# One copy for 1280 scores, another instruction for the second softmax's factor, and norm statistics on GpSimd in a differential-attention layer

## The chip, the cores and the metric

The kernel runs on one core of a Trainium2 chip. TensorE (PE) multiplies matrices into PSUM; its weight loads are listed as PEld. VectorE (DVE), ScalarE (ACT) and GpSimd (POOL) do the elementwise work, and SyncE (SP) issues the DMAs. The metric is the device time of one execution in microseconds (us).

## The reference

A trunk of two layers works on 1024 latent tokens and 256 context tokens of width 1024. Layer 0 mixes tokens with a Fourier transform, layer 1 with differential attention; each layer ends in a SwiGLU feed-forward. The change lies in the attention of layer 1, cut here to what matters:

```python
def diff_attn_core(q, k, v, lam):            # 8 heads, 2 components c of width 64; v has width 128
    s = einsum('bqhcd,bkhcd->bhcqk', q, k) * 64 ** -0.5
    p = softmax(s, axis=-1)                  # over 256 context and 1024 latent keys
    w = p[:, :, 0] - lam * p[:, :, 1]
    return einsum('bhqk,bkhe->bqhe', w, v)

def finish(o):
    o = rms_norm(o, subln_gain) * (1.0 - lam_init)
    return o.reshape(b, l, 1024) @ w_out
```

The subtracted weights are formed without a division of the whole row: with e0 and e1 the exponentials of the two components and r0, r1 their row sums, the kernel uses e0 - lam * (r0 / r1) * e1, which is w times r0. The RMS norm that follows takes r0 out again; its epsilon is therefore multiplied by r0 squared.

## The kernel before

The attention goes over 16 groups, each one head `h` and one half `qg` of the 1024 queries. A group has four query tiles `j` of 128 queries, and each tile has two units, one for each component `c`. `unit(j, c)` (L1006) lets PE write the scores of 128 queries against 1280 keys into PSUM: 1024 columns into a two-bank tile `sc` that rotates through two buffers, and, for both components of the tile at once, 256 columns each into the one bank of `ct`. DVE then copies the scores to SBUF with the sign turned, 1024 columns on L1017 and 256 on L1018; both are accumulating tensor_scalar instructions whose accumulator takes the row's minimum, and each is followed by a small instruction that reads the accumulator out. ACT takes the exponential of all 1280 columns in one instruction and sums the row (L1019).

After the second unit of a tile DVE works out the factor: a reciprocal (L1022), then a scalar_tensor_tensor on a single column (L1023). The second exponential is multiplied by it, on POOL for the tiles in `POOLM` (L1029) and on ACT for the others (L1031), and POOL adds the two (L1032). In the first group the tiles in `RAMP` do both steps on DVE instead (L1025).

The second half of the work on a group runs in ten steps `kt` over the keys (L1184). PE transposes four 128x128 blocks of the weights into a bank `pt` (L1187), ACT and DVE split them into a high and a low part (L55, L56), and PE multiplies them with the values in three matmuls into `po` (L1191 to L1193). Units are issued ahead of this: `advance` (L1190) keeps them three, later five units ahead of the following group's start, so about one unit goes with each `kt`. After the last step `post` copies `po` out (L1046), transposes it back (L1051), copies it on DVE (L1053) and squares it on ACT (L1056), both from the same bank, multiplies epsilon by r0 squared on DVE (L1059), and, once for the two groups of a head, adds the two terms (L1067) and takes the inverse root in eleven small DVE instructions (L60 to L69). POOL then scales the outputs (L1071), and four more transposes (L1078) and an ACT copy (L1082) store them. For the last head each half does this by itself. `oproj0` overlaps the output projection of the first 512 tokens with the last group.

The order on each engine is made by the framework from the program order and its own estimates; a semaphore wait is set for each dependency. PSUM has eight banks of 512 float32 columns: four for the two `sc` buffers, one for `ct`, one for `po`, two for `pt`.

Of the kernel before, what the change touches and what calls it, by code (L numbers as in the profile page):

```python
# [20 lines left out]
P = 128  # L21
# [14 lines left out]
def trunk(tc, a, dbg=None, stop=99):  # L36
# [21 lines left out]
    def rsqrt_ops(y, v, t, steps=3):  # L58
        yi = y.bitcast(I32)
        V.tensor_scalar(yi, v.bitcast(I32), 1, None, op0=ALU.logical_shift_right)  # L60
        yield
        V.tensor_scalar(yi, yi, -1, 0x5F3759DF, op0=ALU.mult, op1=ALU.add)
        yield
        for _ in range(steps):
            V.tensor_tensor(out=t, in0=y, in1=y, op=ALU.mult)
            yield
            V.scalar_tensor_tensor(out=t, in0=t, scalar=-0.5, in1=v, op0=ALU.mult, op1=ALU.mult)
            yield
            V.scalar_tensor_tensor(out=y, in0=t, scalar=1.5, in1=y, op0=ALU.add, op1=ALU.mult)  # L69
            yield  # L70

    def run(*gens):
# [888 lines left out]
    ap = ph4.enter_context(tc.tile_pool(name="ap", bufs=2, reuse_waits="tile"))  # L961
    pss = ph4.enter_context(tc.tile_pool(name="pss", bufs=2, space=PSUM, reuse_waits="tile"))
    pst = ph4.enter_context(tc.tile_pool(name="pst", bufs=2, space=PSUM, reuse_waits="tile"))
# [11 lines left out]
    sg = cst.tile([P, 1], F32, name="sg")  # L975
    V.tensor_scalar(sg, subln, 1.0 - LAM_INIT, None, op0=ALU.mult)

    oT = {}
    pairs = {}
    NE, LEAD, POOLM, RAMP = (11, 3), 5, (1, 2, 3), (1, 3)  # L980

    def load_v(h):
        vs = ap.tile([P, 2, 10, P], F32R, name="v")
        for s in range(2):
            nc.sync.dma_start(r32(vs[:, s]), vD[s, :, h * P:(h + 1) * P].rearrange("(t p) e -> p t e", p=P))
        heads[h].append(vs)

    def qk_units(h, qg):
# [10 lines left out]
        es_ = {}  # L999
        ct = {}  # L1000

# [4 lines left out]
        def unit(j, c):  # L1006
            jsl = slice(j * P, (j + 1) * P)
            col = lambda i: st[:, i, j:j + 1]
            sc = pss.tile([P, 2, 512], F32, name="sc")
            for bk in range(2):  # L1010
                scores(sc[:, bk], c, jsl, slice(bk * 512, (bk + 1) * 512))
            if c == 0:
                ct[j] = pst.tile([P, 2, LC], F32, name="ct", bufs=1)
                for cc in range(2):
                    scores(ct[j][:, cc], cc, jsl, slice(L, T))
            e = ap.tile([P, T], F32, name=f"e{c}", bufs=NE[c])
            V.tensor_scalar(e[:, 0:L], sc.rearrange("p a b -> p (a b)"), -1.0, 3.0e38, op0=ALU.mult, op1=ALU.min, accum_out=col(c))  # L1017
            V.tensor_scalar(e[:, L:T], ct[j][:, c], -1.0, col(c), op0=ALU.mult, op1=ALU.min, accum_out=col(4 + c))  # L1018
            S.activation(out=e, in_=e, func=AF.Exp, scale=-1.0, bias=col(4 + c), accum_out=col(10 + c))  # L1019
            es_[c] = e  # L1020
            if c == 1:
                V.reciprocal(col(12), col(11))  # L1022
                V.scalar_tensor_tensor(out=col(12), in0=col(12), scalar=nlam, in1=col(10), op0=ALU.mult, op1=ALU.mult)  # L1023
                if (h, qg) == (0, 0) and j in RAMP:
                    V.scalar_tensor_tensor(out=es_[0], in0=es_[1], scalar=col(12), in1=es_[0], op0=ALU.mult, op1=ALU.add)  # L1025
                    wts[j] = es_[0]
                    return
                if j in POOLM:
                    G.tensor_tensor(out=es_[1], in0=es_[1], in1=col(12).broadcast_to([P, T]), op=ALU.mult)  # L1029
                else:  # L1030
                    S.activation(out=es_[1], in_=es_[1], func=AF.Copy, scale=col(12))  # L1031
                G.tensor_tensor(out=es_[0], in0=es_[0], in1=es_[1], op=ALU.add)  # L1032
                wts[j] = es_[0]

# [4 lines left out]
    def post(h, qg, po, st):  # L1039
# [8 lines left out]
        def p1():  # L1048
# [9 lines left out]
            z = sn[:, 1, 4 * qg:4 * qg + 4]  # L1058
            V.scalar_tensor_tensor(out=z, in0=st[:, 10], scalar=EPS, in1=st[:, 10], op0=ALU.mult, op1=ALU.mult)  # L1059
            if not both:  # L1060
# [4 lines left out]
        def norm(qs):  # L1065
            s0, s1, s2_, s3 = (sn[:, i, 4 * qs[0]:4 * qs[-1] + 4] for i in range(4))
            V.scalar_tensor_tensor(out=s0, in0=s0, scalar=1.0 / P, in1=s1, op0=ALU.mult, op1=ALU.add)  # L1067
            rsqrt(s2_, s0, s3)
            for q in qs:
# [29 lines left out]
    def advance(target):  # L1099
        nonlocal done  # L1100
        while done < target:
            if not stream:
                n = len(info)
                if n >= len(groups):
                    return
                need(n)
            stream.pop(0)()
            done += 1

    def oproj0():  # L1110
# [26 lines left out]
        for nn in range(NC):  # L1137
# [4 lines left out]
            if nn == 5:  # L1142
                for k in (5, 6):
                    os1(k)
                for i in range(2):
                    nc.sync.dma_start(xt1[i], xres[:, 4 * i:4 * i + 4, 512:1024])
            if nn % 2 == 0:
                acc = pss.tile([P, 2, 512], F32, name="acc", tag="sc")
            pt = acc[:, nn % 2]
            for k in range(NC):  # L1150
# [532 lines left out]
```

## Time and profile before

| | |
|---|---|
| median of three runs | 2795.62 us (2793.28 to 2798.28) |
| profiled execution | 2793.9 us, span of its instructions 2792.1 us |
| granted TensorE clock, mean over the span | 0.987 |
| busy over the span | PE 2664.8 (95%), PEld 2182.4 (78%), DVE 1609.0 (58%), ACT 1106.5 (40%), POOL 960.1 (34%) |
| first and last score copy (L1017) | 1538.6 and 1946.2 us |
| first and last value matmul (L1191) | 1563.8 and 1997.3 us |

The shares are means over stages with different limits; the attention is the only stage in which DVE, and not PE, is busy over nine tenths. Times below count from the span's start. A duration runs from an instruction's start to its end, and neighbours on an engine overlap a little, so the time that an instruction takes from its engine is read from start to start.

### The profile page before, as it was taken

Reading aid. Unit: us, or ns where it says so; the run is one execution under the profiler, and the core shown is the slowest. Engines: PE = TensorE matmul, PEld = TensorE weight load, DVE = VectorE, ACT = ScalarE, POOL = GpSimd, SP = SyncE. Lnnn points to the kernel's source line nnn. Section 1 sums busy time; section 2 is a strip of 40 time slices with the busy share of each in tenths; the row PEclk is TensorE's granted clock in tenths of the full one; section 3 lists DMA queues with packets and bytes.
Section 4 is the critical chain, followed back from the end, with each engine's and each line's share of the span. In section 5 each row is a group of like instructions: output and inputs, shape, how many; then the busy total and the mean of one; then the engine's idle time right before and its main releaser. Section 6 shows DMA issues by size and latency. Waiting matters only on the chain.

```text
span 2792.1 us, 35671 instructions
## 1 busy us (share of the span) xinstructions
PE 2664.8 (95%) x13234; PEld 2182.4 (78%) x13234; DVE 1609.0 (58%) x2920; ACT 1106.5 (40%) x1940; POOL 960.1 (34%) x648
## 2 busy tenths in 40 slices
PE   6999999999999999999999888898987999999999
PEld 4678888888888888878888666676766788888887
DVE  7744644434333434586764999999666555555342
ACT  5642333222322111333343776687434333334231
POOL 4431024221211000013351676777046666651000
PEclk9999999999999999999999999999999999999999
DMA  6682122222222111143335523222243222226352
GB/s 210 203 272 84 31 76 80 84 87 79 88 83 68 39 38 38 50 138 116 114 114 185 157 83 107 83 69 84 80 128 94 87 87 82 82 79 208 109 181 87
DMA packets 284480, 290.64 MB, mean 104 GB/s; under 512 B 16249, under 2 KB 201874, under 8 KB 284306
## 3 DMA queue, kind: packets, MB, share of 16 engines
q1 hardware_dynamic: 282146, 284.69, 32.8%
q0 software_dynamic: 2160, 3.67, 0.4%
q8 instruction: 104, 1.70, 0.3%
q14 instruction: 70, 0.57, 0.1%
HBM read 234.83 MB, written 53.48 MB: 103 GB/s over the span
## 4 chain that ended last, share of the span: by engine, by line
PE 71%; DVE 11%; issue 8%; POOL 6%; DMA 2%; ACT 2%; SPq 0%; POOLq 0%; DVEq 0%; ACTq 0%
PE ps L50 12%; PE ps L52 12%; PE ps L51 12%; PE b L1418 4%; PE b L1416 4%; PE b L1417 4%; PE b L51 3%; PE b L52 3%; PE b L50 3%; DVE e L1017 2%; POOL xn L894 2%; POOL t L895 2%; PE pt L1187 1%; PE ps L229 1%; DVE wt L56 1%
## 5 line engine op out<-in xcount | busy, mean ns | idle before, releaser
L50 PE MATMUL ps<-un,whl 128*128 128x512 f32 x1184 | 464.4, 393 | 1.4 <-ACT XT L592 1.2
L51 PE MATMUL ps<-un,whl 128*128 128x512 f32 x1184 | 461.3, 390 | 0.0
L52 PE MATMUL ps<-un,whl 128*128 128x512 f32 x1184 | 460.9, 389 | 0.0
L56 DVE TENSOR_TENSOR whl<-raw,whl 128x512 fp32r<-128x512 f32 x219 | 170.8, 793 | 271.2 <-ACT whl L55 270.5
L50 PEld LDWEIGHTS ps<-un,whl 128*128 128x128 f32 x1184 | 222.4, 188 | 54.9 <-issue 3.5
L52 PEld LDWEIGHTS ps<-un,whl 128*128 128x128 f32 x1184 | 222.3, 188 | 46.9
L51 PEld LDWEIGHTS ps<-un,whl 128*128 128x128 f32 x1184 | 222.6, 188 | 44.8 <-issue 0.7
L55 ACT ACTIVATE whl<-raw 128x512 fp32r<-128x512 f32 x219 | 134.7, 628 | 246.2 <-PE ps L52 178.1
L736 DVE SCALAR_TENSOR_TENSOR XT<-ps,mods,XT 128x512 f32<-128x512 f32 (+1 forms) x264 | 170.3, 660 | 85.2 <-PE ps L52 84.9
L262 POOL TENSOR_TENSOR acc<-acc,aw 128x512 f32<-128x512 f32 x84 | 112.6, 1340 | 296.4 <-ACT acc L258 231.2
L1032 POOL TENSOR_TENSOR e<-e,e 128x1280 f32<-128x1280 f32 x62 | 182.9, 2951 | 91.3 <-DMA q<-qD 52.8
L1019 ACT ACTIVATE e<-e,st 128x1280 f32<-128x1280 f32 x128 | 174.7, 1366 | 62.0 <-DVE e L1018 45.7
L607 POOL TENSOR_TENSOR nacc<-nacc,s 128x512 f32<-128x512 f32 (+1 forms) x35 | 41.0, 1172 | 414.2 <-ACT s L606 392.7
L51 PE MATMUL ps<-u,whl 128*128 128x256 f32 x592 | 167.5, 283 | 0.0
L52 PE MATMUL ps<-u,whl 128*128 128x256 f32 x592 | 167.4, 283 | 0.0
L50 PE MATMUL ps<-u,whl 128*128 128x256 f32 x592 | 167.3, 283 | 0.0
L1017 DVE TENSOR_SCALAR_CACHE_REDUCE e<-sc 128x1024 f32<-128x1024 f32 x128 | 154.8, 1216 | 10.3 <-PE sc L1004 8.1
L819 PE MATMUL ps<-whl,un 128*128 128x512 f32 x384 | 152.9, 398 | 0.0
L820 PE MATMUL ps<-whl,un 128*128 128x512 f32 x384 | 150.2, 392 | 1.0 <-DVE whl L56 0.9
L821 PE MATMUL ps<-whl,un 128*128 128x512 f32 x384 | 149.9, 391 | 0.0
L51 PE MATMUL b<-au,wu 128*128 128x512 f32 x336 | 130.9, 390 | 0.1
L50 PE MATMUL b<-au,wu 128*128 128x512 f32 x336 | 130.8, 390 | 0.0
(419 smaller groups left out, 6436.3 us busy)
## 6 DMA issues: line engine op xcount, KB each, us to landing
aw<-in_w_ada SPq DMA_DIRECT2D x96, 256.0 KB, 2.8
raw<-in_ffn_w_in SPq DMA_DIRECT2D x88, 256.0 KB, 2.9
wr<-in_ffn_w_out SPq DMA_DIRECT2D x42, 512.0 KB, 4.1
wada<-in_w_ada SPq DMA_DIRECT2D x48, 256.0 KB, 3.3
un<-in_w_ada SPq DMA_DIRECT2D x48, 256.0 KB, 4.5
raw<-in_diff_w_in SPq DMA_DIRECT2D x48, 256.0 KB, 3.5
rq<-in_ffn_w_in SPq DMA_DIRECT2D x24, 512.0 KB, 5.6
raw<-in_ffn_w_out SPq DMA_DIRECT2D x44, 256.0 KB, 2.9
```

Of the source, the lines that this page charges most:

```text
L50: PE.matmul(out, wh, mh, start=start, stop=False)
L51: PE.matmul(out, wh, ml, start=False, stop=False)
L52: PE.matmul(out, wl, mh, start=False, stop=stop)
L55: S.activation(out=hl[:, 0], in_=src, func=AF.Copy)
L56: (lo_eng or V).tensor_tensor(out=hl[:, 1], in0=src, in1=r32(hl[:, 0]), op=ALU.subtract)
L736: V.scalar_tensor_tensor(out=xs, in0=pt, scalar=gmod[c][:, nn:nn + 1], in1=xs, op0=ALU.mult, op1=ALU.add)
L819: PE.matmul(pt, hk[:, 0, tsl], ws[k][:, 0], start=k == 0, stop=False)
L820: PE.matmul(pt, hk[:, 0, tsl], ws[k][:, 1], start=False, stop=False)
L821: PE.matmul(pt, hk[:, 1, tsl], ws[k][:, 0], start=False, stop=k == NC - 1)
L1017: V.tensor_scalar(e[:, 0:L], sc.rearrange("p a b -> p (a b)"), -1.0, 3.0e38, op0=ALU.mult, op1=ALU.min, accum_out=col(c))
L1019: S.activation(out=e, in_=e, func=AF.Exp, scale=-1.0, bias=col(4 + c), accum_out=col(10 + c))
L1032: G.tensor_tensor(out=es_[0], in0=es_[0], in1=es_[1], op=ALU.add)
```

## The change

Scores and PSUM: the rotating tiles `sc` and `ct` go. One tile `sc2` of 2560 columns holds both components: component 0 in columns 0 to 1279, component 1 in 1280 to 2559. That is five banks, and the middle one holds the last 256 columns of component 0 and the first 256 of component 1. PE fills each half in three pieces that end at bank borders (`CUTS`), so a unit still has six matmuls. One DVE instruction copies all 1280 columns.

Factor: it is formed by an accumulating tensor_scalar with two per-row operands, followed by the reading of the accumulator, and no longer by a scalar_tensor_tensor. The whole combination of a tile (factor, product and sum) is put off until after the copy and the exponential of the next unit. `POOLM` goes from tiles 1, 2, 3 to tiles 0 and 2, so ACT multiplies two tiles of a group where it multiplied one.

Norm: the square of r0, its product with epsilon and the sum run on POOL, and so does the inverse root, as a chain of fourteen POOL instructions (`rsqrt_pool`); only the last half of the last head keeps the DVE version. The factor 1/128 moves into the constants.

`oproj0` takes its accumulators from banks 0, 1, 3 and 4 of `sc2`. No DMA is added, removed or moved.

```diff
+    def rsqrt_pool(y, v, t, steps=3):
+        G.tensor_scalar(y.bitcast(I32), v.bitcast(I32), -0.5, float(0x5F3759DF), op0=ALU.mult, op1=ALU.add)
+        G.tensor_scalar(v, v, -0.5, None, op0=ALU.mult)
+        for _ in range(steps):
+            G.tensor_tensor(out=t, in0=y, in1=y, op=ALU.mult)
+            G.tensor_tensor(out=t, in0=t, in1=v, op=ALU.mult)
+            G.tensor_scalar(t, t, 1.5, None, op0=ALU.add)
+            G.tensor_tensor(out=y, in0=y, in1=t, op=ALU.mult)
...
-    V.tensor_scalar(sg, subln, 1.0 - LAM_INIT, None, op0=ALU.mult)
+    V.tensor_scalar(sg, subln, (1.0 - LAM_INIT) * math.sqrt(P), None, op0=ALU.mult)
+    sc2 = pss.tile([P, 2 * T], F32, name="sc2")
+    CUTS = ((0, 512, 1024, T), (0, 256, 768, T))
...
-    NE, LEAD, POOLM, RAMP = (11, 3), 5, (1, 2, 3), (1, 3)
+    NE, LEAD, POOLM, RAMP = (11, 3), 5, (0, 2), (1, 3)
...
-            sc = pss.tile([P, 2, 512], F32, name="sc")
-            for bk in range(2):
-                scores(sc[:, bk], c, jsl, slice(bk * 512, (bk + 1) * 512))
-            if c == 0:
-                ct[j] = pst.tile([P, 2, LC], F32, name="ct", bufs=1)
-                for cc in range(2):
-                    scores(ct[j][:, cc], cc, jsl, slice(L, T))
+            sc = sc2[:, c * T:(c + 1) * T]
+            for k0, k1 in zip(CUTS[c], CUTS[c][1:]):
+                scores(sc[:, k0:k1], c, jsl, slice(k0, k1))
             e = ap.tile([P, T], F32, name=f"e{c}", bufs=NE[c])
-            V.tensor_scalar(e[:, 0:L], sc.rearrange("p a b -> p (a b)"), -1.0, 3.0e38, op0=ALU.mult, op1=ALU.min, accum_out=col(c))
-            V.tensor_scalar(e[:, L:T], ct[j][:, c], -1.0, col(c), op0=ALU.mult, op1=ALU.min, accum_out=col(4 + c))
-            S.activation(out=e, in_=e, func=AF.Exp, scale=-1.0, bias=col(4 + c), accum_out=col(10 + c))
+            V.tensor_scalar(e, sc, -1.0, 3.0e38, op0=ALU.mult, op1=ALU.min, accum_out=col(c))
+            S.activation(out=e, in_=e, func=AF.Exp, scale=-1.0, bias=col(c), accum_out=col(10 + c))
             es_[c] = e
+            while comb:
+                comb.pop()()
             if c == 1:
...
+                comb.append(lambda: combine(j, col, e0, e1))
+
+        def combine(j, col, e0, e1):
+            V.reciprocal(col(12), col(11))
+            V.tensor_scalar(col(13), col(12), col(10), nlam, op0=ALU.mult, op1=ALU.mult, accum_out=col(14))
+            if (h, qg) == (0, 0) and j in RAMP:
+                V.scalar_tensor_tensor(out=e0, in0=e1, scalar=col(14), in1=e0, op0=ALU.mult, op1=ALU.add)
+                return
+            if j in POOLM:
+                G.tensor_tensor(out=e1, in0=e1, in1=col(14).broadcast_to([P, T]), op=ALU.mult)
+            else:
+                S.activation(out=e1, in_=e1, func=AF.Copy, scale=col(14))
+            G.tensor_tensor(out=e0, in0=e0, in1=e1, op=ALU.add)
...
-            V.scalar_tensor_tensor(out=z, in0=st[:, 10], scalar=EPS, in1=st[:, 10], op0=ALU.mult, op1=ALU.mult)
+            G.tensor_tensor(out=z, in0=st[:, 10], in1=st[:, 10], op=ALU.mult)
...
-            V.scalar_tensor_tensor(out=s0, in0=s0, scalar=1.0 / P, in1=s1, op0=ALU.mult, op1=ALU.add)
-            rsqrt(s2_, s0, s3)
+            G.tensor_scalar(s1, s1, P * EPS, None, op0=ALU.mult)
+            G.tensor_tensor(out=s0, in0=s0, in1=s1, op=ALU.add)
+            (rsqrt if qs == (1,) else rsqrt_pool)(s2_, s0, s3)
...
-            if nn % 2 == 0:
-                acc = pss.tile([P, 2, 512], F32, name="acc", tag="sc")
-            pt = acc[:, nn % 2]
+            c0 = (0, 512, T + 256, T + 768)[nn % 4]
+            pt = sc2[:, c0:c0 + 512]
```

## Rows read from the trace of the kernel before

**Rows 1.** Busy time by stage: length; PE, PEld, DVE, ACT, POOL; clock; DMA share, GB/s.

```profile
1563.80:1618.00 54.20, 50.01 (x268) 39.65 (x268) 53.08 (x128) 44.07 (x74) 44.61 (x17) 1.00 0.23 70
1618.00:1889.00 271.00, 238.34 (x1261) 187.86 (x1260) 255.50 (x580) 196.63 (x370) 198.76 (x81) 0.96 0.31 88
```

**Rows 2.** Source line L1017 over the whole run: durations min/median/max, first, last.

```profile
L1017 DVE TENSOR_SCALAR_CACHE_REDUCE e<-sc x128: 1198/1216/1226, 1538.6 to 1946.2; 128x1024 f32<-128x1024 f32 x128
```

**Rows 3.** DVE groups, 1618 to 1889 us: count, busy, mean ns, idle before, releaser.

```profile
L1017 DVE TENSOR_SCALAR_CACHE_REDUCE e<-sc 128x1024 f32<-128x1024 f32 x80 | 97.0, 1217 | 7.4 <-PE sc L1004 6.1 <-PE pt L1187 0.9
...
L1018 DVE TENSOR_SCALAR_CACHE_REDUCE e<-ct,st 128x256 f32<-128x256 f32 x80 | 37.6, 475 | 2.8 <-PE ct L1004 2.6
L1023 DVE SCALAR_TENSOR_TENSOR st<-st,nlam 128x1 f32<-128x1 f32 x41 | 22.9, 559 | 0.1
L1059 DVE SCALAR_TENSOR_TENSOR sn<-st 128x4 f32<-128x4 f32 x10 | 9.8, 980 | 0.0
L69 DVE SCALAR_TENSOR_TENSOR sn<-sn 128x8 f32<-128x8 f32 x15 | 8.6, 575 | 0.0
...
L62 DVE TENSOR_SCALAR sn<-sn 128x8 int32<-128x8 int32 x5 | 2.6, 511 | 0.0
```

**Rows 4.** Source lines L1023 and L1022, same stretch: durations min/median/max ns.

```profile
L1023 DVE SCALAR_TENSOR_TENSOR st<-st,nlam x41: 200/215/2190, 1618.7 to 1888.4; 128x1 f32<-128x1 f32 x41
...
L1022 DVE RECIPROCAL st<-st x40: 145/158/165, 1626.9 to 1885.0; 128x1 f32<-128x1 f32 x40
```

**Rows 5.** Timeline, 1717 to 1722.5 us: start, us, engine, instruction, idle and releaser.

```profile
1717.57 2.96 POOL L1032 TENSOR_TENSOR e<-e,e 128x1280 f32<-128x1280 f32 x1 [2.46 <-ACT e L1031]
...
1718.09 2.45 DVE L1059 SCALAR_TENSOR_TENSOR sn<-st 128x4 f32<-128x4 f32 x1
...
1720.95 1.20 DVE L1017 TENSOR_SCALAR_CACHE_REDUCE e<-sc 128x1024 f32<-128x1024 f32 x1
...
1722.21 0.50 PE L1003 MATMUL sc<-k,q 128*128 128x512 f32 x1 [1.64 <-DVE e L1017]
```

**Rows 6.** Timeline, 1711 to 1713.5 us: DVE's and PE's starts.

```profile
1711.53 1.21 DVE L1017 TENSOR_SCALAR_CACHE_REDUCE e<-sc 128x1024 f32<-128x1024 f32 x1
...
1711.84 0.28 PE L1004 MATMUL ct<-k,q 128*128 128x256 f32 x1
...
1711.96 0.40 PE L1193 MATMUL po<-wt,v 128*128 128x512 f32 x1
...
1712.19 0.60 PE L1187 MATMUL pt<-ident,e 128*128 128x128 f32 x4
...
1712.55 0.47 PE L1004 MATMUL sc<-k,q 128*128 128x512 f32 x1
...
1712.66 0.68 DVE L56 TENSOR_TENSOR wt<-pt,wt 128x512 fp32r<-128x512 f32 x1
1712.86 0.39 PE L1191 MATMUL po<-wt,v 128*128 128x512 f32 x1
```

**Rows 7.** ACT groups, 1618 to 1889 us.

```profile
L1031 ACT ACTIVATE e<-e,st 128x1280 f32<-128x1280 f32 x10 | 13.6, 1362 | 6.2 <-DVE sn L67 4.5 <-DVE st L1023 1.2 <-DVE sn L69 0.5
L1056 ACT ACTIVATE jk<-pt 128x128 bf16<-128x128 f32 x40 | 10.5, 278 | 4.8 <-DVE on L1053 4.8
```

**Rows 8.** POOL groups, 1618 to 1889 us.

```profile
L1029 POOL TENSOR_TENSOR e<-e,st 128x1280 f32<-128x1280 f32 x30 | 69.7, 2323 | 30.6 <-DVE st L1023 17.2 <-DVE sn L67 3.3 <-ACT e L1019 2.7
L1071 POOL TENSOR_TENSOR on<-on,sn 128x512 f32<-128x512 f32 x10 | 10.2, 1042 | 16.6 <-DVE sn L69 15.7 <-DVE st L1022 0.8
```

**Rows 9.** Timeline, 1724.6 to 1726.2 us: the second and fourth `ct` matmul, and L1018.

```profile
1724.93 0.28 PE L1004 MATMUL ct<-k,q 128*128 128x256 f32 x1
...
1725.17 0.28 PE L1004 MATMUL ct<-k,q 128*128 128x256 f32 x1
...
1725.49 0.48 DVE L1018 TENSOR_SCALAR_CACHE_REDUCE e<-ct,st 128x256 f32<-128x256 f32 x1 [0.24 <-PE ct L1004]
```

**Rows 10.** Source line L549, POOL instructions on two columns: durations min/median/max ns.

```profile
L549 POOL CAST un<-y0hl x8: 190/192/193, 137.3 to 138.2; 128x2 fp32r<-128x2 f32 x8
```

More of the change, by code (lines that the diff above doesn't have):

```diff
@@ L961, in trunk @@
     ap = ph4.enter_context(tc.tile_pool(name="ap", bufs=2, reuse_waits="tile"))
-    pss = ph4.enter_context(tc.tile_pool(name="pss", bufs=2, space=PSUM, reuse_waits="tile"))
+    pss = ph4.enter_context(tc.tile_pool(name="pss", bufs=1, space=PSUM, reuse_waits="tile"))
     pst = ph4.enter_context(tc.tile_pool(name="pst", bufs=2, space=PSUM, reuse_waits="tile"))
@@ L986, in load_v @@
         heads[h].append(vs)
+    comb = []
     def qk_units(h, qg):
@@ L999, in qk_units @@
         es_ = {}
-        ct = {}
         def scores(out, c, jsl, ksl):
@@ L1020, in unit @@
+            S.activation(out=e, in_=e, func=AF.Exp, scale=-1.0, bias=col(c), accum_out=col(10 + c))
             es_[c] = e
+            while comb:
+                comb.pop()()
             if c == 1:
[L1022 to L1033, printed above, removed]
+                e0, e1 = es_[0], es_[1]
+                wts[j] = e0
+                comb.append(lambda: combine(j, col, e0, e1))
[10 more added lines that the diff above has]
+            G.tensor_tensor(out=e0, in0=e0, in1=e1, op=ALU.add)
@@ L1104, in advance @@
                 if n >= len(groups):
+                    while comb:
+                        comb.pop()()
                     return
```

## The prediction, made before the change was run

> **What bounds the kernel now.** I read the busy time by stage first. PE leads over the whole run, but in the attention DVE is busy 255.5 of 271.0 us and PE 238.3 [rows 1]. A stage goes by its own limit, so I counted work per unit. In this stretch DVE copies 80 units [rows 3]: 271.0 / 80 = 3.39 us a unit, DVE 3.19, PE 2.98, ACT 2.46, POOL 2.48. DVE's limit is exceeded by 6%; in the two groups before it, where no norm runs, DVE is busy 53.08 of 54.20 us, an excess of 2% [rows 1]. The last unit starts at 1946.2 us [rows 2], so (1946.2 - 1889) / 3.39 = 17 more run at this pace, 97 in all.
>
> Next, the groups of DVE instructions, for what fills the 3.19 us. Instructions on one to eight columns have means of 0.4 to 1.4 us, L1023 0.559 and L1059 0.980 [rows 3], although L1023 can do it in 0.200 [rows 4]. The timeline shows why: L1059 starts 0.52 us after a POOL sum and ends at 1720.54 us, as the sum does at 1720.53 [rows 5]. The one-operand reciprocal on the same columns stays between 145 and 165 ns all 40 times [rows 4], and the score copies, which read PSUM, vary little [rows 2]. So while POOL works on SBUF, DVE stands at instructions with two SBUF inputs, and at the plain tensor_scalar of the inverse root. The Trainium skill says the same under "SBUF — State Buffer", section "Who interferes with whom": a VectorE instruction with two SBUF inputs waits for a GpSimd instruction that reads SBUF, while the accumulating tensor_scalar does not take the shared port pair. The first half agrees with L1059; no run before shows the second half on SBUF operands. The sum below doesn't use it.
>
> **The parts.** Stalls: eight groups, the first L1023 and the last L62 of [rows 3], hold 111 instructions and 67.9 us. Unhindered they take 41 x 0.205 + 70 x 0.155 = 19.2 us [rows 4]. The stalls are 48.7 us, 0.61 us a unit. Fourteen and a half are L1023's, 41 x (0.559 - 0.205). The norm's 70 instructions also leave DVE: starts show 0.08 us of occupancy each, 0.07 a unit.
>
> The copy: 768 columns separate 1217 from 475 ns, 0.97 ns each [rows 3], so 1280 columns take 1.217 + 0.25 = 1.46 us in place of 1.69. Starts overlap by 0.08 us for an instruction (L1017 frees DVE after 1.13 of its 1.21 us [rows 6]), so the saving is 0.15 a unit. The accumulating factor is shown nowhere on one column: below it lies L1022's 0.158, above it L1018's 0.475 [rows 3, 4] against 0.205 now; nearest in size is the first, with an accumulator read of 0.08 I take +0.05 a unit at most. DVE comes to 3.19 - 0.61 - 0.07 - 0.15 + 0.05 = 2.41.
>
> ACT multiplies one more tile a group, 10 x 1.36 = 13.6 us in the stretch [rows 7], and comes to 2.63. POOL loses 10 x 2.32 [rows 8] and gets 18 small instructions a head, 90 here. None is shown on eight columns; on two columns it is 0.19 [rows 10], on 512 it is 1.04 [rows 8]. The small end is by far nearer: 90 x 0.19 = 17 us, POOL 2.41. At the other end it would be 94 us and 3.36. The copy of the first component no longer finds its factor work queued behind it; the factor comes a unit, some 3 us, later, and is hidden by the five units of lead, about 15 us. Without that cover each tile would cost PE up to 3 us. No DMA moves, and SP's and POOL's queues pass none.
>
> PE's work doesn't change. From starts [rows 6]: 512 columns 0.23, 256 columns 0.12, four transposes 0.36, the matmul behind them 0.08 more. A unit's scores are 4 x 0.23 + 2 x 0.12 = 1.16; a step over the keys is 0.36 + 0.08 + 3 x 0.23 = 1.13, 1.25 of them a unit; the norm's transposes add 0.1. Together 2.67 us. PE would be the bound, not DVE.
>
> **The middle bank.** PE would be free to reach it if the two halves of the new tile were independent, but they share a bank. Two readings show that this framework orders accesses by bank. L1018 of a first component needs the first two `ct` matmuls, which end at 1725.21; DVE is idle from 1725.25 and starts at 1725.49, after the fourth, which writes the other component's columns, ends at 1725.45 [rows 9]. And the squares on ACT (L1056) wait 4.8 us for the copy L1053 [rows 7], though both only read the same bank. So the second unit of a tile, whose first piece lies in the middle bank, can't begin before the first unit's copy is done, and the first unit's last piece can't before the second's copy of the tile ahead. Per tile: copy 1.46, PE starts 0.06 after it (1722.15 to 1722.21 [rows 5]), the second unit 2 x 0.12 + 3 x 0.23 + 0.40 = 1.33 to the end of its last matmul, 0.04 to DVE's start [rows 9]: 2.89. Then copy 1.46 + 0.06 + last piece 0.12 + 0.28 + 0.04 = 1.96. The chain is 4.85 us a tile. PE has 5.34 us of work, 1.40 of it in the chain's own PE legs; 3.94 must go beside the two copies, where there are 2 x 1.56 = 3.12. The remaining 0.82 stretches the tile to 5.67, a unit to 2.83. With the excess that this stretch has now, 6%, it is 3.00.
>
> **Sum.** 97 x (3.39 - 3.00) = 38 us. The two groups ahead gain about 2 by the same chain (DVE loses little there, being 98% busy on unhindered copies). The first tiles and the last norm lose about 3: the first tile's product is on POOL at 2.32 instead of ACT at 1.36 [rows 7, 8], its factor waits for another exponential, and the last half-head hops to POOL and back. Net 37 us off the profiled 2793.9, which has its own time as base: 2757. The median of the runs is 1.7 us above that execution, so I forecast 2758 us.
>
> **The rivals.** *PE free of the bank* (13%): if the waits went by columns, PE's 2.67 x 1.06 = 2.83 would hold: 97 x 0.56 = 54, net 53, 2743 us. At an excess of 2% it is 2.72 a unit, 65 us, 2732. Against it stand the two readings above.
>
> *The accumulating form stalls as well* (9%): its operands lie in SBUF, as L60's did, and L60 has one tensor input [rows 3]. Then L1023's 14.5 us stay, 0.18 a unit, and fall into the chain: 97 x 0.18 = 17, 2775 us. For the forecast speaks that the reciprocal never stalls.
>
> *POOL late* (8%): the norm of a head is a burst of 18 small instructions and two of 1.04. At 0.19 it takes 5.5 us, within the lead; at 1.04 each it takes 21 us and PE waits for the sums queued behind it, some 6 us in each of seven heads by the lead's 15: 42 us. Half of that gives 2779, all of it 2800.
>
> *The ping-pong binds* (15%), the one on the other side. Place: the middle bank, twice a tile. Each in-order queue may put other work ahead of the released instruction. The tile takes 6.78 us now, the chain 4.85, so 1.93 us of inserted work decide; I forecast 1.15. If DVE puts one split (0.6 of L56 [rows 6]) ahead of each copy and PE a whole step (1.13) ahead of the second unit, it is 4.85 + 1.2 + 1.13 = 7.18, 3.59 a unit: 97 x 0.20 = 19 us more, with the 3 of the ends 2818. This is where a rule of the Trainium skill speaks against the change: "PSUM — Partial Sum Buffer", section "PSUM bank collisions raise a hardware error", asks for guarding PSUM by bank and quadrant and not by address, and the trace agrees with rows 9. Up to 1.9 us of inserted work the change still wins, and DVE has slack for it, 2.41 against 3.00 a unit.
>
> **How the numbers follow.** Forecast 55%, the four rivals as given. About 0.2% or 5.6 us is what a measurement of this kernel can tell from no change. Faster: the forecast, the first two rivals and most of the POOL case, 0.82. Same: parts of the POOL case and of the ping-pong near its threshold, 0.06. Slower: the rest of the ping-pong, 0.12. The range goes from 2735, just short of PE's limit at 2%, to 2793; the losing ping-pong and the worst POOL case lie outside. The forecast's own range, at excesses from 2% to 10%, is 2746 to 2770.
>
> **What would show it.** L1059, L1067 and the DVE inverse root are gone up to the last half-head, and the new factor instruction has a maximum near its median (a maximum over 1 us: the second rival). Copies of about 1.46 us, 128 of them, one accumulator read each. DVE's busy share in the stage falls from 94% to about 80%, PE's rises above 89%. The first matmul of a second unit follows the end of the first unit's copy by 0.06 us, and waits of PE's score matmuls on that copy lead the list; if they start during the copy, the first rival holds. Small POOL instructions over 0.5 us, or transposes waiting long for L1032's successor, would show POOL late. The last score copy starts near 1909 us after the span's start instead of 1946. The prediction is wrong if that start moves by under 10 us, or if it moves and a later stage gives the time back.

## The result, and the profile after

The changed kernel takes 2836.27 us (median of 4 runs, 2834.32 to 2837.66) against 2796.95 us for the kernel before beside it: ratio 1.0141, 95% interval 1.0124 to 1.0159. I had forecast 2758 us with a range to 2793. It is slower by 1.4% where I expected 1.3% faster.

The busy time by stage, with the columns of [rows 1], shows that DVE did get faster and that this is not where the time went.

```profile
1542.40:1583.40 41.00, 24.00 (x62) 16.50 (x62) 18.61 (x35) 13.50 (x19) 10.51 (x5) 0.50 0.52 156
...
1618.00:1889.00 271.00, 240.70 (x1244) 181.98 (x1243) 201.32 (x391) 210.82 (x379) 193.12 (x161) 1.00 0.29 88
```

In the stretch from 1618 us DVE was busy 255.5 us before [rows 1] and is busy 201.3 now, with one copy more. No engine is full there any more: PE 89%, ACT 78%, DVE 74%, POOL 71%. When every engine has slack and the pace doesn't rise, the limit is a chain that goes round through several engines. The group of copies in that stretch (count, busy, mean, idle before, releaser) says where DVE stands in it.

```profile
L1027 DVE TENSOR_SCALAR_CACHE_REDUCE e<-sc 128x1280 f32<-128x1280 f32 x81 | 120.8, 1492 | 51.3 <-PE sc L1018 50.0
```

The copy waits 50 us for the last score matmul; the copies of [rows 3] waited 6.1 us for theirs. The list of waits of the same stretch (total, times, longest) has the other half of the circle: the score matmuls wait for the copy.

```profile
DVE e L1027 <- PE sc L1018: 50.0, 66, 1.5
PEld sc L1017 <- DVE e L1027: 39.4, 67, 1.6
...
PE sc L1017 <- DVE e L1027: 18.7, 26, 1.4
```

Where PE has nothing else to do the circle stands bare. This is the timeline at the start of the attention, PE's and DVE's lines alone.

```profile
1546.23 1.49 DVE L1027 TENSOR_SCALAR_CACHE_REDUCE e<-sc 128x1280 f32<-128x1280 f32 x1 [2.33 <-PE sc L1018]
...
1547.78 0.79 PE L1017 MATMUL sc<-k,q 128*128 128x512 f32 x1 [1.59 <-DVE e L1027]
...
1549.87 0.41 PE L1018 MATMUL sc<-k,q 128*128 128x256 f32 x1
...
1550.32 1.49 DVE L1027 TENSOR_SCALAR_CACHE_REDUCE e<-sc 128x1280 f32<-128x1280 f32 x1 [2.59 <-PE sc L1018]
...
1551.88 0.58 PE L1017 MATMUL sc<-k,q 128*128 128x256 f32 x1 [1.59 <-DVE e L1027]
...
1553.75 0.63 PE L1018 MATMUL sc<-k,q 128*128 128x512 f32 x1
...
1554.41 1.49 DVE L1027 TENSOR_SCALAR_CACHE_REDUCE e<-sc 128x1280 f32<-128x1280 f32 x1 [2.20 <-PE sc L1018]
```

Read it by the shapes. The unit that begins with a 512-column piece at 1547.78 is a first component: its first piece fills columns 0 to 511, the first bank. The copy that it waits 1.59 us for, from 1546.23, reads columns 1280 to 2559, banks 2 to 4. The two share no bank. The second component (256 columns first, at 1551.88) waits for the copy ahead of it in the same way. So copy and matmuls never overlap, 4.09 us a unit here. Later, at full clock, it is the same with other PE work between.

Where the 43.8 us between the profiled spans (2792.1 and 2835.9) arose can be read from the starts of the first value matmul of each half-head's group, ten a group in order. The columns: from the first score copy to the first value matmul; groups 1 and 2; groups 3 to 14, and that by their 96 units; from group 15 to the last value matmul; all us. Seven more kernels, told of below, stand beside the two.

```
kernel                       first copy    copy to    groups   groups   a unit   groups
                             starts        value mm   1, 2     3-14              15, 16
before                       1538.6        25.2       54.2     322.8    3.36     56.6
after                        1542.1        41.5       60.0     331.6    3.45     63.5
old scores (e1)              1544.1        26.8       49.3     284.5    2.96     57.2
fillers (e5)                 1542.3        29.2       58.3     331.4    3.45     63.3
bank waits (e6)              1540.8        28.5       50.3     279.4    2.91     57.6
factor alone (e7)            1539.5        25.2       53.1     309.3    3.22     54.9
norm alone (e8)              1540.6        25.4       55.5     308.9    3.22     57.6
factor and norm (e9)         1543.1        24.6       52.0     274.7    2.86     56.4
fourth buffer (e11)          1540.1        26.8       49.2     271.1    2.82     57.1
```

The start gives 16.3 us of the loss, groups 1 and 2 give 5.8, the twelve in the middle 8.8, the last two 6.9 (the output projection accumulates in the same score tile now, but so it does in e6, with 57.6, so that is not what costs the time); 3.5 lie ahead of the first copy, where e1's is later still, and 2.4 behind the attention.

### The profile page after: what moved, and what is told of

It reads as the page before. It is cut to its first block, busy times and chain, and to the rows that moved or that the text cites. A ratio compares the mean times of both kernels' runs of the same rounds, so it can differ in the third digit from the quotient of the medians.

```text
span 2835.9 us, 35405 instructions
## 1 busy us (share of the span) xinstructions
PE 2692.4 (95%) x13234; PEld 2191.5 (77%) x13234; DVE 1533.9 (54%) x2615; ACT 1126.8 (40%) x1954; POOL 958.1 (34%) x780
## 4 chain that ended last, share of the span: by engine, by line
PE 75%; issue 8%; DVE 6%; POOL 6%; ACT 2%; DMA 2%; SPq 0%; POOLq 0%; DVEq 0%; ACTq 0%
PE ps L50 12%; PE ps L52 12%; PE ps L51 12%; PE b L1433 4%; PE b L1435 4%; PE b L1434 4%; PE b L51 3%; PE b L52 3%; PE b L50 3%; PE sc L1017 3%; DVE e L1027 3%; PE sc L1018 2%; POOL xn L904 2%; POOL t L905 1%; PE pt L1204 1%
## 5 line engine op out<-in xcount | busy, mean ns | idle before, releaser
L1027 DVE TENSOR_SCALAR_CACHE_REDUCE e<-sc 128x1280 f32<-128x1280 f32 x128 | 190.9, 1492 | 97.1 <-PE sc L1018 94.4
L1017 PE MATMUL sc<-k,q 128*128 128x512 f32 (+1 forms) x384 | 153.4, 405 | 41.1 <-DVE e L1027 38.3
L1017 PEld LDWEIGHTS sc<-k,q 128*128 128x128 f32 x384 | 75.6, 197 | 83.2 <-DVE e L1027 71.2
```

What stands on the lines that cost most here:

```text
L1017: PE.matmul(out, qs[:, c, 0, jsl], ks[c][:, ksl], start=True, stop=False)
L1027: V.tensor_scalar(e, sc, -1.0, 3.0e38, op0=ALU.mult, op1=ALU.min, accum_out=col(c))
```

## The experiments

**The score layout put back (e1), and put in alone (e2).** e1 is the changed kernel with the score tiles and the two copies of before; the factor, the later combination and the norm on POOL stay. e2 is the kernel before with the new score tile and the single copy and nothing else of the change.

```diff
 # e1, against the changed kernel (e2: the same lines the other way, in the kernel before)
-            sc = sc2[:, c * T:(c + 1) * T]
-            for k0, k1 in zip(CUTS[c], CUTS[c][1:]):
-                scores(sc[:, k0:k1], c, jsl, slice(k0, k1))
+            sc = pss.tile([P, 2, 512], F32, name="sc")
+            for bk in range(2):
+                scores(sc[:, bk], c, jsl, slice(bk * 512, (bk + 1) * 512))
...
-            V.tensor_scalar(e, sc, -1.0, 3.0e38, op0=ALU.mult, op1=ALU.min, accum_out=col(c))
+            V.tensor_scalar(e[:, 0:L], sc.rearrange("p a b -> p (a b)"), ...
+            V.tensor_scalar(e[:, L:T], ct[j][:, c], -1.0, col(c), ...
```

> The change with the scores' PSUM layout and the two copies of before (two rotating tiles and the shared bank); factor, delay, tile split and norm stay as changed. Theory H (the hold is on the whole tile: the first matmul of a unit waits for the copy of the unit just before it, because both halves lie in one tile): PE and DVE overlap again, DVE has 2.41 + 0.15 = 2.56 us a unit and PE 2.67, with 6 to 10% excess 2.83 to 2.94, so 2740 to 2760 us, and the TensorE clock in the first 40 us of the attention is back at 1.0. Rival R1 (the rest of the change costs the time: later factors, the norm on POOL, one more product on ACT): 2796 to 2840 us. Rival R2 (hold by the shared middle bank, as in the prediction): as H here.

> The kernel before with only the one tile for all scores and its single copy; factor, timing and norm as before. H: the serial hold and the stalls of VectorE both count, so slower than the changed kernel or as slow: 2835 to 2890 us, half clock at the start of the attention. R1: the copy saves 0.15 us a unit and nothing else changes: 2775 to 2790 us. R2: as H, with the first pieces of a first component starting before the copy of the second component is done.

e1: 2757.59 us, 0.9858 (0.9843 to 0.9873). e2: 2860.22 us, 1.0225 (1.0209 to 1.024). The score layout is the whole loss, and more: without it the rest of the change gains 1.4%, and alone it loses 2.3%. That the forecast's 2758 and e1 agree is chance; e1 has none of the chain through the middle bank that the forecast was added up from.

**What holds the matmuls: whole banks (e3) and two tiles (e4).** e3 gives each component three banks of its own inside one tile; e4 makes them two tiles. Both take six banks for the scores in place of five, so both have one transpose buffer (`pt`) in place of two.

```diff
 # e3, against the changed kernel
-    pst = ph4.enter_context(tc.tile_pool(name="pst", bufs=2, space=PSUM, ...
+    pst = ph4.enter_context(tc.tile_pool(name="pst", bufs=1, space=PSUM, ...
-    sc2 = pss.tile([P, 2 * T], F32, name="sc2")
+    sc2 = pss.tile([P, 2, 1536], F32, name="sc2")
+    scs = [sc2[:, c] for c in range(2)]
 # e4, against e3
-    sc2 = pss.tile([P, 2, 1536], F32, name="sc2")
-    scs = [sc2[:, c] for c in range(2)]
+    scs = [pss.tile([P, 1536], F32, name=f"sc{c}") for c in range(2)]
```

> The changed kernel with the two halves on three banks each (no shared bank), still one tile of six banks; the transposes' PSUM tile goes from two buffers to one to make room. H: the hold stays, since it goes by the tile, and the transposes wait more: 2835 to 2900 us. R2: the hold is gone, and the time is that of the next kernel within 0.3%.

> As the kernel before it in this list, but with the two halves as two tiles of three banks each; the same banks, the same instructions. H: a unit's matmuls start while the other component is copied, faster than the one tile by 40 us or more: 2760 to 2800 us. R2: the same time as the one tile of six banks within 0.3%. R1: no faster than 2796 us.

e3: 2981.11 us, 1.0658. e4: 3073.18 us, 1.0993. Both are slower than the changed kernel and slower than I expected, so as times they don't tell the theories apart. The single transpose buffer is the likely reason, but no run took it by itself, and why e4 is slower than e3 stays open. In e4 the copies wait for POOL's sums, which free the rows of `e`, and no longer lead with a wait for a score matmul (the copy's source line over the whole run):

```profile
its engine sat idle before it (us, times) until:
  POOL e L1048: 139.9, 41
  PE sc L1018: 52.4, 37
```

What can be used is the start, where the transposes hardly matter yet: the first value matmul comes at 1580.4 us in e3, 39.3 us after the first copy, and at 1565.0 in e4, 26.6 after it. Separate banks change little (41.5 in the changed kernel); separate tiles bring the 25.2 of before nearly back. The timelines of the start show the hold itself, first of e3, then of e4.

```profile
1541.06 1.49 DVE L1028 TENSOR_SCALAR_CACHE_REDUCE e<-sc 128x1280 f32<-128x1280 f32 x1 [1.00 <-DMA v<-vD]
...
1542.62 0.50 PE L1018 MATMUL sc<-k,q 128*128 128x512 f32 x1 [1.59 <-DVE e L1028]
```

```profile
1539.78 1.49 DVE L1027 TENSOR_SCALAR_CACHE_REDUCE e<-sc 128x1280 f32<-128x1280 f32 x1
...
1539.92 0.50 PE L1017 MATMUL sc<-k,q 128*128 128x512 f32 x1 [0.51 <-DVE e L1027]
```

In e3 the second component's first piece waits 1.59 us for the end of the first component's copy, with which it shares no bank. In e4 the first piece of the next tile starts 0.14 us into the other component's copy; what it waited for is the copy of its own component, just ended. Counted over the whole traces, none of the 768 score matmuls starts while a score copy runs in the changed kernel, in e2 and in e3, but 133 do in e4. The hold goes by the tile, not by the bank.

**The waits by bank (e6).** The changed kernel, with the wait declared needless for every 512-column piece against the other component's copy. Those pieces lie in banks 0, 1, 3 and 4. The two 256-column pieces, which share bank 2, keep their wait and are written last in both units.

```diff
-            for k0, k1 in zip(CUTS[c], CUTS[c][1:]):
-                scores(sc[:, k0:k1], c, jsl, slice(k0, k1))
+            for k0, k1 in ((0, 512), (512, 1024), (1024, T)) if c == 0 else ((256, 768), (768, T), (0, 256)):
+                for s in range(2):
+                    m = PE.matmul(sc[:, k0:k1], qs[:, c, s, jsl], ks[c][:, k0:k1], start=s == 0, stop=s == 1)
+                    if k1 - k0 == 512 and 1 - c in copied:
+                        tc.declare_no_dep(m.ins, copied[1 - c].ins, reason="other banks")
-            V.tensor_scalar(e, sc, ...
+            copied[c] = V.tensor_scalar(e, sc, ...
```

> The changed kernel, same tile and same copy, but the matmuls into the four banks that one component has to itself are declared independent of the other component's copy, and the pieces in the shared bank come last in both units. Theory H (the waits of the changed kernel go by the whole tile): PE writes one component while DVE copies the other, the chain of the shared bank is 2 x (1.46 + 0.06 + 0.12 + 0.28 + 0.04) = 3.92 us a tile, below PE's 5.34, and a unit takes 2.83 to 2.94 us: 2735 to 2760 us, clock 1.0 at the start. Rival R2 (the shared bank holds the units anyway): within 0.3% of the changed kernel's 2836 us.

2757.49 us, 0.9868 (0.985 to 0.9885): the whole loss is gone, 82.5 us of span against the changed kernel, for the same matmuls, copies and bytes. Now 269 of the 768 score matmuls start while a score copy runs. Its timeline shows the overlap that was missing, and the one hold that is left.

```profile
1689.43 1.49 DVE L1031 TENSOR_SCALAR_CACHE_REDUCE e<-sc 128x1280 f32<-128x1280 f32 x1 [0.59 <-PE sc L1027]
...
1689.93 0.85 PE L1027 MATMUL sc<-k,q 128*128 128x512 f32 x3
...
1690.99 0.73 PE L1027 MATMUL sc<-k,q 128*128 128x256 f32 x3 [0.21 <-DVE e L1031]
```

The 512-column pieces start 0.50 us into the other component's copy; the 256-column piece waits for its end at 1690.92. By stage PE is the bound, busy 264 of 271 us:

```profile
1618.00:1889.00 271.00, 263.97 (x1461) 210.31 (x1460) 230.51 (x453) 244.92 (x446) 224.94 (x191) 1.00 0.35 101
```

The Trainium skill's rule that the prediction cited, from "PSUM — Partial Sum Buffer", section "PSUM bank collisions raise a hardware error", to guard by bank and quadrant, describes e6: between the components it waits in the shared bank alone. The changed kernel waits for more than that rule asks.

Two comparisons go with this. e1, with two copies and all else alike, stands at 0.9858, so with the hold gone one copy in place of two gains nothing that these runs can tell. And e6 is the nearest to what the prediction took the change to be; that its 2757 meets the forecast of 2758 is in part luck, since its order of pieces has a shorter chain through the bank, 3.92 us a tile where the prediction had 4.85, and its unit takes 2.91 us and not 3.00.

**The start (e5).** The changed kernel with six matmuls of 512 columns behind each of the first eleven units, into a spare transpose tile that nothing reads. They add work that the result doesn't need.

```diff
+            if len(fill) < 11:
+                fill.append(pst.tile([P, 512], F32, name="pt"))
+                for _ in range(6):
+                    PE.matmul(fill[-1], qs[:, c, 0, jsl], ks[c][:, 0:512], start=True, stop=True)
```

> The changed kernel with six more matmuls of 512 columns behind each of the first eleven units, into a transposes' bank that nobody reads: work that isn't needed, put into the waits of PE at the start of the attention. Theory C (the serial hold leaves PE idle half of the time there, the clock falls to its lower level, and every unit takes 4.1 us instead of 3.0): the clock stays at 1.0, the first value matmul comes 10 to 14 us earlier than the changed kernel's 1583.6 us, and the time is 2822 to 2828 us. Rival (the start is late through the hold and POOL alone, the clock doesn't matter): first value matmul within 3 us of 1583.6, 2833 to 2840 us.

2824.44 us, 1.0103. In the changed kernel the granted clock is 0.50, the lower level of 1.2 GHz, over the 41.0 us that the first fence shows, with PE busy 24.0 of them and idle for a copy in every unit. With the fillers it is 1.00 until the first value matmul:

```profile
1542.40:1571.40 29.00, 27.02 (x128) 21.13 (x126) 19.02 (x35) 13.62 (x20) 10.64 (x5) 1.00 0.75 223
```

From first copy to first value matmul it takes 29.2 in place of 41.5 us. So 12.3 of the 16.3 us lost at the start go with the slower clock in the idle circle, measured by a kernel that has more to compute. The middle groups don't change, 331.4 us: there the granted clock was 1.00 anyway.

**The two stall edits, singly (e7, e8) and together (e9).** All are the kernel before with its own score layout and nothing delayed.

```diff
 # e7
-                V.scalar_tensor_tensor(out=col(12), in0=col(12), scalar=nlam, in1=col(10), op0=ALU.mult, op1=ALU.mult)
+                V.tensor_scalar(col(13), col(12), col(10), nlam, op0=ALU.mult, op1=ALU.mult, accum_out=col(14))
 # e8
...
-            V.scalar_tensor_tensor(out=s0, in0=s0, scalar=1.0 / P, in1=s1, op0=ALU.mult, op1=ALU.add)
-            rsqrt(s2_, s0, s3)
+            G.tensor_scalar(s1, s1, P * EPS, None, op0=ALU.mult)
+            G.tensor_tensor(out=s0, in0=s0, in1=s1, op=ALU.add)
+            (rsqrt if qs == (1,) else rsqrt_pool)(s2_, s0, s3)
 # e9: both
```

> The kernel before with the factor by the accumulating form alone; no delay, old tiles, old norm. Stall theory: L1023's 14.5 us of stalls in 80 units go, 0.18 us a unit over 97 units: 2775 to 2785 us, and the new instruction keeps near 0.27 us at most. Rival (the stall moves to the next instruction with two SBUF inputs, or PE and POOL take it up): within 0.2% of before.

> The kernel before with the norm statistics on POOL alone. Stall theory: 34 us of stalls and 6 us of own time leave DVE in the stretch of 80 units, 0.50 us a unit; PE's limit then stops the gain, 2.83 to 3.0 us a unit: 2742 to 2765 us. Rival (POOL's chains hold up the sums that PE waits for): 2785 to 2810 us.

> The kernel before with both stall edits (the accumulating factor and the norm statistics on POOL), the old score layout, nothing delayed. Theory: a POOL instruction on SBUF holds whichever two-SBUF-input instruction stands next in DVE's queue. With the factor alone the inverse root's first instructions rose to 1.99 us each, with the norm alone the factor rose from 0.56 to 0.95 us, so each alone only moves part of the stall; together nothing is left to hold, and the gain is more than the sum of the two. Expected 2754 to 2764 us, ratio 0.986 to 0.989. Rival: the two stalls are separate and simply add, ratio 0.9944 + 0.9964 - 1 = 0.9908, 2769 us. A second reading: the gap to the kernel with the old scores and all the rest of the change (0.9858) is what the later combination is worth; expected within 4 us of nothing.

e7: 2780.12 us, 0.9944 (0.9929 to 0.996). e8: 2785.22 us, 0.9964 (0.9951 to 0.9977), a much smaller gain than I expected. e9: 2747.24 us, 0.9827 (0.9812 to 0.9842), below the range that I expected. In groups 3 to 14 the factor alone gains 13.5 us, the norm alone 13.9, both 48.1. The DVE groups of the stretch of [rows 3] show where the stalls go, first in e8, then in e7:

```profile
L1033 DVE SCALAR_TENSOR_TENSOR st<-st,nlam 128x1 f32<-128x1 f32 x42 | 40.0, 951 | 0.1
```

```profile
L62 DVE TENSOR_SCALAR sn<-sn 128x8 int32<-128x8 int32 x6 | 11.9, 1988 | 0.0
L1023 DVE TENSOR_SCALAR_CACHE_REDUCE st<-st,nlam 128x1 f32<-128x1 f32 x41 | 11.0, 267 | 0.2
L1059 DVE SCALAR_TENSOR_TENSOR sn<-st 128x4 f32<-128x4 f32 x12 | 7.6, 646 | 0.0
...
L69 DVE SCALAR_TENSOR_TENSOR sn<-sn 128x8 f32<-128x8 f32 x15 | 4.9, 330 | 0.0
```

With the norm gone, the factor that stays stands 0.951 us in place of 0.559 [rows 3]: 42 x (0.951 - 0.205) = 31 us are held there, where it was 14.5. So about half of the 34 us of stall that the norm's instructions took comes back on the factor.

The other way round it does not. With the factor gone, the inverse root's L62 stands 1.99 us in place of 0.51, but L1059 stands 0.65 in place of 0.98 and L69 0.33 in place of 0.58. All of the norm's DVE instructions together take 48.3 us in 76 in e7 and took 45.0 us in 70 before, 0.64 us each both times: which of them is held changes, not how much. e7 gains 0.14 us a unit of the 0.18 that the factor's stall was worth.

So what is missing singly is missing in e8: there DVE's work falls from 3.19 to 2.89 us a unit, with both edits to 2.60, and the gain of both is larger than the sum of the two. The rival, that the two gains add to 0.9908, is out. Left open is why e8 turns only 0.14 us of those 0.30 into time.

**The later combination (e10, e11, e12).** e9 is ahead of e1 by 0.9858 - 0.9827, some 9 us, where I expected at most 4. e1 differs from it by the later combination and by the tiles whose product is on ACT, 1 and 3 in place of 0. e10 is e6 with each tile of the first group combined in its own unit again and tile 0's product on ACT. e11 is e1 with four buffers for the second component's rows. e12 is e6 without the delay in any group, tiles 1 to 3 on POOL as before.

```diff
 # e10, against e6
                 comb.append(lambda: combine(j, col, e0, e1))
+                if (h, qg) == (0, 0):
+                    comb.pop()()
...
-            if j in POOLM:
+            if j in POOLM and (h, qg, j) != (0, 0, 0):
 # e11, against e1
-    NE, LEAD, POOLM, RAMP = (11, 3), 5, (0, 2), (1, 3)
+    NE, LEAD, POOLM, RAMP = (11, 4), 5, (0, 2), (1, 3)
 # e12, against e6
-    NE, LEAD, POOLM, RAMP = (11, 3), 5, (0, 2), (1, 3)
+    NE, LEAD, POOLM, RAMP = (11, 3), 5, (1, 2, 3), (1, 3)
-                comb.append(lambda: combine(j, col, e0, e1))
+                combine(j, col, e0, e1)
```

> The kernel with the waits of the separate banks taken away, and in the first group alone each tile is combined in its own unit again and tile 0 is multiplied on ACT. Theory: there PE waits 2.4 us twice for POOL's sums before the first value matmul (1569.3 us against 1563.8 in the kernel before), since the sum of a tile now comes a unit later and tile 0's product is on POOL at 2.32 instead of ACT at 1.36 us; expected first value matmul at 1564 to 1566 us and 3 to 5 us less in all, 2752 to 2755 us. Rival: the start is set by the copies, whose chain runs through the shared bank, and nothing changes, 2757 us.

> All of the change but the score layout, with four buffers in place of three for the second component's rows (e1). Theory: the later combination holds a tile's e1 a unit longer, so the copy of a second component waits for POOL's sum of three tiles before (14.4 us in nine waits between 1618 and 1889 us, against 5.1 in four where both stall edits stand without the delay); with a fourth buffer these waits go and the time comes to that of the two stall edits alone, 2745 to 2750 us, ratio 0.982 to 0.984. Rival: what the delay and the two products on POOL in place of three cost is ACT's added product, and the buffer changes nothing: 2756 to 2759 us, ratio 0.986.

> The kernel with the waits of the separate banks taken away, each tile combined in its own unit in every group and tiles 1 to 3 multiplied on POOL as in the kernel before: the one copy of 1280 scores and the two stall edits, without the delay. Theory: PE's work bounds both score layouts once the hold is gone (2.85 to 2.9 us a unit), so it lands beside the two stall edits alone, 2744 to 2751 us, ratio 0.981 to 0.984. Rival: the delay is what lets the copies of one unit follow each other without the factor between, and without it the time is 2756 us or more.

e10: 2755.69 us, 0.9861 (0.9845 to 0.9878). From first copy to first value matmul it takes 25.7 in place of 28.5 us, near what the theory said, but the total moves by 0.0007, less than can be told from nothing. e12: 2755.55 us, 0.9862: here my theory missed, and without the delay nothing changes in this layout.

e11: 2740.12 us, 0.9802 (0.9788 to 0.9817), the fastest of all and 2% below the kernel before. The waits tell what the buffer did. In e1, between 1618 and 1889 us:

```profile
DVE e L1030 <- POOL e L1052: 14.4, 9, 4.4
```

In e11, the same copy's source line over the whole run, with what ended its waits:

```profile
  PE pt L1209: 8.7, 10
  PE sc L1017: 4.1, 6
  POOL e L1049: 0.2, 1
```

The wait for POOL's sum falls from 14.4 us to 0.2. A tile's second row of `e` is freed by that sum; when the sum comes a unit later, three buffers are too few. The rival, that the buffer changes nothing, is out. With four, PE is busy 267.1 of the 271 us:

```profile
1618.00:1889.00 271.00, 267.12 (x1510) 217.74 (x1508) 248.07 (x661) 249.28 (x460) 232.11 (x194) 1.00 0.36 102
```

## Why the prediction was wrong

**The step that failed is "The middle bank".** It says "this framework orders accesses by bank", and lets only the pieces in the shared bank wait: 4.85 us a tile. The waits go by the whole tile, so the first component's two 512-column pieces wait as well and every unit is copy, then matmuls, with no overlap. The timeline of the changed kernel at full clock shows a unit in which PE puts no other work between its first and last score matmul:

```profile
1719.09 1.49 DVE L1027 TENSOR_SCALAR_CACHE_REDUCE e<-sc 128x1280 f32<-128x1280 f32 x1 [0.58 <-PE sc L1018]
...
1720.65 0.50 PE L1017 MATMUL sc<-k,q 128*128 128x512 f32 x1
...
1721.79 0.28 PE L1018 MATMUL sc<-k,q 128*128 128x256 f32 x1
...
1722.11 1.49 DVE L1027 TENSOR_SCALAR_CACHE_REDUCE e<-sc 128x1280 f32<-128x1280 f32 x1 [0.92 <-PE sc L1018]
```

From copy to copy it is 3.02 us. A tile's chain is then 6.04 us, and 3.45 x 2 = 6.90 is what it takes, with 0.86 of other PE work and waits put between. The forecast had allowed 1.15 for those, on a chain of 4.85. The chain alone leaves 0.74 of the 6.78 that a tile took before, where the prediction thought it had 1.93 to spare.

The two readings behind that step could not have told the cases apart. In [rows 9] the `ct` tile is one bank, and in [rows 7] L1056 and L1053 share a `pt` tile of one bank: bank and tile are the same thing in both. A tile of two banks stood in the trace of before, and I didn't look at it: `acc` in the output projection. Its rows in the timeline of the kernel before:

```profile
2019.97 0.39 PE L52 MATMUL acc<-os,wo 128*128 128x512 f32 x1
...
2020.40 0.75 DVE L1160 SCALAR_TENSOR_TENSOR xt<-acc,mods,xt 128x512 f32<-128x512 f32 x1 [1.36 <-PE acc L52]
...
2021.30 0.47 PE L50 MATMUL acc<-os,wo 128*128 128x512 f32 x1 [0.93 <-DVE xt L1160]
```

DVE reads one half of `acc`, a bank of its own, until 2021.15; the matmul that opens the other half starts at 2021.30, after 0.93 us of waiting for it. By that row both units of a tile run the prediction's longer leg of 2.89 us, and the chain is 5.78 us, near the 6.04 measured.

**The start was mis-sized.** "The first tiles and the last norm lose about 3": 16.3 us to the first value matmul and 6.9 in the last two groups. The circle leaves PE idle in a stretch with nothing else to run, and the granted clock there is 0.50: the six matmuls of a unit take 2.50 us (1547.78 to 1550.28) where at full clock they take 1.42 (1720.65 to 1722.07). e5 puts this at 12.3 us. The forecast had no term for the clock.

**The stalls were right.** L1059, L1067 and the inverse root have left DVE but for the last half-head, and the factor never stalls. Its source line over the whole run, min, median and max:

```profile
L1040 DVE TENSOR_SCALAR_CACHE_REDUCE st<-st,nlam x64: 259/270/276, 1551.9 to 1987.5; 128x1 f32<-128x1 f32 x64
```

The next DVE instruction starts 0.19 us after it, where it was 0.13 after an unhindered L1023: 0.06 more, near the 0.05 allowed. This settles the rival "The accumulating form stalls as well", and the half of the rule that no run before showed: by the Trainium skill, "SBUF — State Buffer", section "Who interferes with whom", the accumulating tensor_scalar does not take the shared port pair, and 64 of 64 agree, on operands in SBUF. Two readings were loose without harm: the means of the small instructions go down to 0.31 us (L65), not 0.4, and [rows 3] show L62's single input, not L60's. DVE's work a unit came to 201.32 / 81 = 2.49 us against 2.41; the copy to 1.49 against 1.46. What the stalls were worth e9 shows: 3.36 falls to 2.86 us a unit, where PE is busy 264 of 271 us and becomes the bound.

**POOL was right.** Small instructions take 0.20 to 0.24 us on eight columns, near the 0.19 that I chose and far from 1.04:

```profile
L79 POOL TENSOR_SCALAR sn<-sn 128x8 f32<-128x8 f32 x15 | 3.5, 235 | 1.3
...
L77 POOL TENSOR_TENSOR sn<-sn 128x8 f32<-128x8 f32 x15 | 3.0, 200 | 0.8
```

**PE was right.** 2.67 us a unit, 2.83 with its excess: 2.82 in e11, 2.86 in e9, 2.91 in e6. The 2743 us of "PE free of the bank" lies between e11 and e9, 2740 and 2747, which have no hold but two copies, and e11 a fourth buffer.

**The delay was costed at nothing, for the wrong reason.** "Hidden by the five units of lead" looked at PE, which does not wait for the factor. What ran out was buffers on the other side: three `e1` rows. In the changed kernel no copy waits for a POOL sum, so there it cost nothing beside the hold. With the two copies, e1 against e9 puts the delay and the other split of the products at some 9 us, and the fourth buffer is worth 0.9858 - 0.9802, some 16 us, with the delay; no run has it without. With one copy (e6 against e12) the delay costs nothing.

The rival "The ping-pong binds" named the right side and the right circle, at 15%, but put its place in one bank and its threshold more than twice too high. Of the signs listed, DVE's busy share fell below the 80% I gave (74%), PE's stayed at 89%, the score matmuls' waits on the copy do lead on PE, and the last score copy starts at 1983.6 us, not 1909.

Left open: why one copy of 1280 scores with waits by bank (e6, e10, e12, all at 2.91 us a unit) stays 0.05 to 0.09 us a unit behind e9 and e11, two copies with the same stalls gone, though it is ahead of e1 at 2.96. The shared bank still holds (in e6 copies wait 25 us for score matmuls in the stretch), but no run took that alone away.

## What to carry to other kernels

Before packing two buffers into one tile to save an instruction, find in the trace a tile that spans several banks and see whether a writer of one part waits for a reader of another; a reading on a one-bank tile can't say. Price the packed layout as a circle (copy, release, matmuls, release), compare it with the pace of today, and ask what PE's clock does where the circle leaves it idle. Two kinds of instruction that stall on the same partner are best taken away together, and a result that is consumed a unit later can need a buffer more.

## What was not expected of the hardware

A stall that is taken from one kind of instruction can come back on another: with the norm gone from DVE, the factor's mean rose from 0.56 to 0.95 us, and the two removals, 0.6% and 0.4% singly, give 1.7% together. It need not: with the factor gone, the norm's instructions take 0.64 us each as before, though L62 alone rose from 0.51 to 1.99. Matmuls that nobody needs made a kernel faster: 66 extra ones at the start raised the granted clock there from 0.50 to 1.00 and brought the ratio from 1.0141 to 1.0103.
